# Three changes of order in a two-layer recurrent decoder kernel: an interleaved start, a state output that leaves later, and a spread set-up product

## The chip, the core and the metric

The kernel runs on one core of a Trainium2 chip. The metric is the device time of one execution in microseconds (us); lower is better. The core has a matrix engine (PE, with weight loads shown apart as PEld), a vector engine (DVE), a scalar engine (ACT), a general engine (POOL) and a sync engine (SP), which in this kernel does little but issue DMAs. Each engine works through its own instructions in their order and waits on semaphores where it needs another engine's result.

## The reference, cut

The program computes one inference step of a decoder trunk of two layers for 256 prompt tokens and 8 sequences of 8 sample tokens, 320 columns in all, at a model width of 2048.

```
def _rmsnorm(x, g): return x * lax.rsqrt(jnp.mean(x * x, axis=-1, keepdims=True) + NORM_EPS) * g
...
# per layer, xn = RMSNorm(x), one combined input projection of xn (N_IN = 14336 columns):
#   A: S5      b_bar = ((lam_bar - 1) / lam) * b ; h_t = lam_bar * h_(t-1) + b_bar u_t ; y = c h + d u
#              y = gelu(y) ; y = y * sigmoid(y @ w_glu + b_glu) ; h_last is an output
#   B: RG-LRU  conv of width 4, block-diagonal gates, h_t = a_t h_(t-1) + sqrt(1 - a_t^2) (i_t xc_t)
#   C: RetNet retention, 8 heads, chunks of 128, GroupNorm per head ; the last states are outputs
# x = x + W_out( sum_m sigmoid(gate_m(xn)) * (P_m(branch_m(xn) * silu(z_m))) )
# a final RMSNorm gives y_prompt, y_sample
```

S5 has 64 groups of 16 channels with a complex state of 64 each, and its recurrence runs over the tokens.

## The kernel before, in words

**The stream.** Almost all of the work is dense projections. `blocks()` yields them one after another as blocks of 256 output columns, each with its weights, its number of 128-row pieces of the contraction, the function that gives the moving operand, and the function that evacuates the result. `stream()` cuts the blocks into chunks of four such pieces. There are 312 chunks in a layer, 624 in all. In layer order: input blocks for the RG-LRU's input and gate path and S5's input (48 chunks), the RG-LRU's merge with its gates (48), the retention heads (64), S5's gate path (16), the second merge (48), S5's GLU (8), the third merge (48), the output projection (32).

For every chunk the program loads 512 KB of raw fp32 weights (`load`, L1211, three chunks ahead, into four `raw` buffers, all on SP's queue). In two halves it splits them into a rounded high part (ACT copy, `whi`, L126) and the rest (DVE subtraction, `wlo`, L99), three halves ahead of use (`prep`). PE then does 24 matmuls of 128x320 in three products (L1273 to L1275) into a PSUM tile `pt`. The evacuation of a block is run one chunk after the block's last.

**The background.** Everything else is written as Python generators, which the program advances between chunks: a `yield` means "the rest one chunk later", `yield 2` two chunks later. `step()` advances all of them after each chunk. So a generator's yields set the order of the instructions on every engine, and a wait in it is a loop on a flag that an earlier generator sets, decided when the program is written, not on the chip.

**The parts that the change touches.** `s5_setup` computes S5's discretized input matrix `bb` with 12 products on POOL (`cmul`) and sets the flag on which `s5_weights` and the chain wait. `s5_chain` runs the recurrence over pairs of tokens on POOL, 127 iterations of four small instructions (`cstep`, L555 to L558), in place in `H`. The sample tokens' recurrence is 8 groups of four instructions on DVE (tiles `cb1`, `cb2`), a group in every second step. Behind the last iteration, two POOL copies (L588) gather the last states into `so`, a DMA on SP's queue (L589) writes them out, and `s5_y` follows when the fourth retention pair has its state (the flag `('st', l, 3)`).

At the start, `x_load` brings x in four groups of two DMAs, `x_group` scales it by the norm's weights and splits it, `norm_feed` gathers the sum of squares. The first two blocks run interleaved. `norm_end` sums over partitions on PE (L259) and works out 1/rms, which the blocks' evacuations need. In the last output blocks, `out_proj` sums the squares for the final norm with a matmul by ones (L1081) at block 6 and two more at block 7.

Of the kernel before, what the change touches and what calls it, by code (L numbers as in the profile page):

```python
# [11 lines left out]
F32 = mybir.dt.float32  # L12
# [3 lines left out]
OP = mybir.AluOpType  # L16
# [5 lines left out]
T = SEQ + NB * NS  # L22
# [3 lines left out]
C_U5, C_Z5, C_UL, C_ZL, C_Q, C_K, C_V, C_ZR = (i * W for i in range(8))  # L26
# [54 lines left out]
class Program:  # L81
# [173 lines left out]
    def norm_end(self):  # L255

        yield
        p = self.ps()
        self.nc.tensor.matmul(p[:, :T], self.ones, self.acc, start=True, stop=True)  # L259
        r = self.rstd = self.pl.tile([128, T], F32, name="rstd", tag="rstd")  # L260
        yield from self.rsqrt_steps(p, r)

    def rsqrt_steps(self, p, r):
        v = self.vt([128, T])
        t = self.vt([128, T])
        self.ts(v, p[:, :T], 1.0 / D, OP.mult, EPS, OP.add)
        self.act(t, v, AF.Ln)
        self.act(r, t, AF.Exp, scale=-0.5)
        yield
        self.mul(t, r, r)  # L270
        self.stt(t, t, -0.5, v, OP.mult, OP.mult)
        self.stt(r, t, 1.5, r, OP.add, OP.mult)
# [9 lines left out]

    def x_load(self, q):
        a = self.py.tile([128, 4, T], F32, name="xin", tag="y")
        for h in range(2):
            self.nc.sync.dma_start(a[:, 2 * h:2 * h + 2], self.I['x'][2 * q + h])
        self.xin[q] = a

    def x_group(self, q):

# [29 lines left out]
    def s5_setup(self, l):  # L320
# [10 lines left out]
        B = []  # L331
# [80 lines left out]
        def cmul(r, xr, xi, yr, yi):  # L412
            yr, yi = (v[:, :, None].to_broadcast([128, 32, 16]) for v in (yr, yi))
            o = [t[:, :, :, r] for t in bb]
            g.tensor_tensor(o[0], xr, yr, op=OP.mult)
            g.tensor_tensor(tmp, xi, yi, op=OP.mult)
            g.tensor_tensor(o[0], o[0], tmp, op=OP.subtract)
            g.tensor_tensor(o[1], xi, yr, op=OP.mult)
            g.tensor_tensor(tmp, xr, yi, op=OP.mult)
            g.tensor_tensor(o[1], o[1], tmp, op=OP.add)  # L420
        cmul(1, B[0], B[1], cre, cim)
        cmul(0, bb[0][:, :, :, 1], bb[1][:, :, :, 1], lamr, ni)
        self.bb = bb
        self.flag['bb', l] = True

# [141 lines left out]
    def s5_chain(self, l):  # L567
        nc, H, g = self.nc, self.H, self.nc.gpsimd
        g.memset(H[:, :, :, 0], 0.0)
        lr2 = self.l2r[:, :, None].to_broadcast([128, 32, 2])  # L570
        for j in range(1, HP):
            self.cstep(H[:, :, :, j + 1], H[:, :, :, j], lr2, self.l2i, [128, 32, 2])
        sh = [128, 32, NB]
        cols = H[:, :, :, HP + 1:].rearrange("p q c (b e) -> p q c b e", e=5)
        for i in range(4):
            for c in range(2):
                old, oth, new = cols[:, :, c, :, i], cols[:, :, 1 - c, :, i], cols[:, :, c, :, i + 1]
                t1 = self.vt(sh, name="cb1")
                t2 = self.vt(sh, name="cb2")
                self.mul(t1, old, self.l2r[:, :, None].to_broadcast(sh))  # L580
                self.mul(t2, oth, self.l2i[:, :, c:c + 1].to_broadcast(sh))
                self.add(t1, t1, t2)
                self.add(new, new, t1)
                yield 2
        yield int(HP * 1.43 / 3.26) - 16
        so = self.wt([128, 2, 32, NB + 1], name="so")
        for c in range(2):
            g.tensor_copy(so[:, c], H[:, :, c, HP:HP + 41:5])  # L588
        nc.sync.dma_start(self.O['s5'][l], so)  # L589
        while not self.flag.get(('st', l, 3)):  # L590
            yield
        yield from self.s5_y(l)
        self.flag['s5done', l] = True

# [461 lines left out]
    def out_proj(self, l, j, pt):  # L1056
        nc = self.nc
        xo = self.xo.pop(j)
        if l + 1 < DEPTH:
            self.add(xo, pt[:, :, :T], xo)  # L1060
            nc.sync.dma_start(self.xs[l + 1][j], xo)
            for n in range(2):
                k = 2 * j + n
                self.norm_feed(k, xo[:, n], self.pcol(l + 1, 'norm', k))
            if j == 5:
                self.table_of(AF.Ln)
            if j == 7:
                yield from self.norm_end()
            return
        pool, tag = (self.pmg, "mg") if j % 2 else (self.py, "y")  # L1070
        y = self.ytok[j] = pool.tile([128, 2, T], F32, name="yt", tag=tag)
        if j < 7:
            self.add(y, pt[:, :, :T], xo)
            for n in range(2):
                self.sumsq(y[:, n])
                self.copy(y[:, n], y[:, n], scale=self.pcol(l, 'fin', 2 * j + n))
            if j == 5:
                self.table_of(AF.Ln)
            if j == 6:
                p = self.fsum = self.ps()  # L1080
                self.nc.tensor.matmul(p[:, :T], self.ones, self.acc, start=True, stop=False, skip_group_check=True)  # L1081
            return
        sq = self.wt([128, 2, T], name="sq")
        for n in range(2):
            self.add(y[:, n], pt[:, n, :T], xo[:, n])
            if n:
                self.mul(sq[:, 1], y[:, 1], y[:, 1])
            else:
                self.act(sq[:, 0], y[:, 0], AF.Square)
        for n in range(2):  # L1090
            self.nc.tensor.matmul(self.fsum[:, :T], self.ones, sq[:, n], start=False, stop=n == 1,  # L1091
                                  skip_group_check=True)
# [21 lines left out]
    def blocks(self):  # L1114
        I = self.I
        for l in range(DEPTH):
# [9 lines left out]
            def inp(col, fn, *a):  # L1126
                return (w_in[col // 256], 16, xn, fn, a)

            yield ('call', self.layer_start, (l,))
            for j in range(4):  # L1130
                yield inp(C_UL + 256 * j, self.lru_u, l, j)
                yield inp(C_ZL + 256 * j, self.silu_z, l, self.szl, 'zl', j)
                yield inp(C_U5 + 256 * j, self.s5_u, l, j)
            yield ('call', self.s5_begin, (l,))
            yield from self.merge_blocks(l, 0, inp, wb['lru'], yb, C_GL)
# [22 lines left out]
    def merge_blocks(self, l, br, inp, wb, yb, cg):  # L1158
        def br_blk(j):
            return (wb[j], 8, yb, self.merge, (br, j))  # L1160
        yield inp(cg, self.gate, 0)
        for j in range(1, 8):
            yield inp(cg + 256 * j, self.gate, j)
            yield br_blk(j - 1)
        yield br_blk(7)

    def layer_start(self, l):
        self.nl = 0
# [24 lines left out]
    def stream(self, ahead=3, halves=3):  # L1193
        nc = self.nc
        chunks, calls, nblk = [], {}, 0
        for b in self.blocks():
# [3 lines left out]
            for c in range(b[1] // 4):  # L1200
                chunks.append((nblk, c, b))
            nblk += 1
        first = [x for p in zip(chunks[0:4], chunks[4:8]) for x in p]
        chunks[:8] = first
        raw, hl, pts = {}, {}, {}

        def load(i):
            if i < len(chunks):
                _, c, b = chunks[i]
                t = self.praw.tile([128, 4, 256], F32, name="raw", tag="raw")  # L1210
                nc.sync.dma_start(t, b[0][:, 4 * c:4 * c + 4])  # L1211
                raw[i] = t

        def prep(u):
            i, h = divmod(u, 2)
# [8 lines left out]
        def run(fn, a, now=False):  # L1224
            g = fn(*a)
            if hasattr(g, '__next__'):
                e = self.spawn(g, 0.5 if fn == self.lru_u else 0)
                if now:
                    self.advance(e)
                    e[1] += 1  # L1230
# [3 lines left out]
                run(fn, a)  # L1234

        self.constants()
        self.x_load(0)
        load(0)
        self.more_constants()
        load(1)  # L1240
        self.x_load(1)
        load(2)
        load(3)
        self.x_load(2)
        self.norm_begin()
        for u, _ in enumerate(self.x_group(0)):
            prep(u)
        prep(2)
        self.x_load(3)
        norm = self.norm_end()  # L1250
        done = []
        for i, (nb, c, b) in enumerate(chunks):
            if i:
                load(i + ahead)
            if c == 0:
                call(nb)
                pts[nb] = self.pmain.tile([128, 2, 512], F32, name="pt", tag="pt")
            if i in (1, 3, 4):
                for _ in self.x_group((0, 1, 0, 2, 3)[i]):
                    pass  # L1260
            nk, pt = b[1], pts[nb]
            for h in range(2):
                if (i, h) in ((5, 0), (6, 1), (7, 0)):
                    next(norm, None)
                prep(2 * i + h + halves)
                hi, lo = hl.pop(2 * i + h)
                for n in range(2):
                    for kk in range(2):
                        k = 4 * c + 2 * h + kk
                        xh, xl = b[2](0, k), b[2](1, k)  # L1270
                        o = pt[:, n, :T]
                        cs = slice(n * 128, (n + 1) * 128)
                        nc.tensor.matmul(o, hi[:, kk, cs], xh, start=k == 0, stop=False)  # L1273
                        nc.tensor.matmul(o, hi[:, kk, cs], xl, start=False, stop=False)  # L1274
                        nc.tensor.matmul(o, lo[:, kk, cs], xh, start=False, stop=k == nk - 1)  # L1275
            if i < 5 and i != 2:
                self.x_rest((0, 1, 0, 2, 3)[i])

            if done and i >= done[0][0]:
                run(*done.pop(0)[1:], now=True)  # L1280
            self.step()
            if c == nk // 4 - 1:
                done.append((i + 1, b[3], b[4] + (pts.pop(nb),)))
        for d in done:
            run(*d[1:])
        while self.gens:
# [99 lines left out]
```

## Time and profile before

| | us |
|---|---|
| median of 3 runs | 2486.08 (2485.41 to 2488.9) |
| time of the profiled execution | 2483.85 |
| its span (first to last instruction) | 2482.1 |

| engine | busy us | share | instructions |
|---|---|---|---|
| PE | 2383.9 | 96% | 16762 |
| DVE | 1558.6 | 63% | 2892 |
| ACT | 1068.4 | 43% | 1932 |
| POOL | 618.3 | 25% | 1157 |

The time is 1.75 us above the span, for what lies around the first and last instruction. The shares are averages over the whole span; which engine the others wait for in a stretch has to be read from that stretch.

### The profile page before, as it was taken

Reading aid. Unit: us, or ns where it says so; the run is one execution under the profiler, and the core shown is the slowest. Engines: PE = TensorE matmul, PEld = TensorE weight load, DVE = VectorE, ACT = ScalarE, POOL = GpSimd, SP = SyncE. Lnnn points to the kernel's source line nnn. Section 1 sums busy time; section 2 is a strip of 40 time slices with the busy share of each in tenths; the row PEclk is TensorE's granted clock in tenths of the full one; section 3 lists DMA queues with packets and bytes.
Section 4 is the critical chain, followed back from the end, with each engine's and each line's share of the span. In section 5 each row is a group of like instructions: output and inputs, shape, how many; then the busy total and the mean of one; then the engine's idle time right before and its main releaser. Section 6 shows DMA issues by size and latency. Waiting matters only on the chain. (4 is left out here: it accounts for less than half of the span.)

```text
span 2482.1 us, 44329 instructions
## 1 busy us (share of the span) xinstructions
PE 2383.9 (96%) x16762; PEld 2330.9 (94%) x16762; DVE 1558.6 (63%) x2892; ACT 1068.4 (43%) x1932; POOL 618.3 (25%) x1157
## 2 busy tenths in 40 slices
PE   7999999999599999999999999999959999999996
PEld 7998999999499999999999999999959999999996
DVE  7788557777365656855567665767736647555543
ACT  5654444333133444444455554433323334444443
POOL 2003006999402000300100000799930200000001
PEclk9999999999799999999999999999979999999998
DMA  5654775455254545455555587454434455444553
GB/s 189 190 172 156 213 223 159 152 179 169 77 170 164 190 153 173 151 160 188 188 166 188 161 226 201 150 177 157 134 130 164 155 186 163 150 148 150 162 173 108
DMA packets 153446, 413.71 MB, mean 167 GB/s; under 512 B 18576, under 2 KB 59280, under 8 KB 152976
## 3 DMA queue, kind: packets, MB, share of 16 engines
q1 hardware_dynamic: 152512, 410.58, 52.1%
q8 instruction: 131, 2.15, 0.4%
q14 instruction: 83, 0.68, 0.1%
q10 hardware_dynamic: 720, 0.30, 0.0%
HBM read 373.83 MB, written 31.74 MB: 163 GB/s over the span
## 5 line engine op out<-in xcount | busy, mean ns | idle before, releaser
L99 DVE TENSOR_TENSOR wlo<-raw,whi 128x512 fp32r<-128x512 f32 x1248 | 883.1, 723 | 872.4 <-ACT whi L126 849.9
L126 ACT ACTIVATE whi<-raw 128x512 fp32r<-128x512 f32 x1248 | 776.2, 629 | 1201.9 <-PE pt L1274 1011.8
L1273 PE MATMUL pt<-xh,whi 128*128 128x320 f32 x3584 | 1128.6, 315 | 11.6 <-ACT whi L126 7.3
L1275 PE MATMUL pt<-xh,wlo 128*128 128x320 f32 x3584 | 1112.8, 311 | 7.5 <-DVE wlo L99 7.3
L1274 PE MATMUL pt<-xl,whi 128*128 128x320 f32 x3584 | 1111.7, 310 | 0.0
L1273 PEld LDWEIGHTS pt<-xh,whi 128*128 128x128 f32 x3584 | 676.5, 189 | 26.8 <-ACT whi L126 15.1
L1275 PEld LDWEIGHTS pt<-xh,wlo 128*128 128x128 f32 x3584 | 675.9, 189 | 9.6 <-DVE wlo L99 9.6
L1274 PEld LDWEIGHTS pt<-xl,whi 128*128 128x128 f32 x3584 | 676.5, 189 | 1.7
L1273 PE MATMUL pt<-yhl,whi 128*128 128x320 f32 x768 | 238.8, 311 | 0.0
L1275 PE MATMUL pt<-yhl,wlo 128*128 128x320 f32 x768 | 237.6, 309 | 0.0
L1274 PE MATMUL pt<-yhl,whi 128*128 128x320 f32 x768 | 237.6, 309 | 0.0
L555 POOL TENSOR_TENSOR cs<-H,l2r 128x64 f32<-128x64 f32 x254 | 127.2, 501 | 256.6 <-DVE H L113 236.8
L252 POOL TENSOR_TENSOR acc<-acc,sq 128x320 f32<-128x320 f32 x28 | 25.5, 911 | 609.3 <-ACT sq L126 608.3
L1273 PE MATMUL pt<-M,whi 128*128 128x320 f32 x512 | 159.4, 311 | 0.0
L1275 PE MATMUL pt<-M,wlo 128*128 128x320 f32 x512 | 159.1, 311 | 0.0
L1274 PE MATMUL pt<-M,whi 128*128 128x320 f32 x512 | 159.0, 311 | 0.0
L1273 PEld LDWEIGHTS pt<-yhl,whi 128*128 128x128 f32 x768 | 144.3, 188 | 1.9 <-issue 1.6
L1274 PEld LDWEIGHTS pt<-yhl,whi 128*128 128x128 f32 x768 | 144.3, 188 | 0.0
L1275 PEld LDWEIGHTS pt<-yhl,wlo 128*128 128x128 f32 x768 | 144.2, 188 | 0.0
L558 POOL TENSOR_TENSOR H<-cs,cs 128x64 f32<-128x64 f32 x254 | 128.6, 506 | 19.9
L556 POOL TENSOR_TENSOR cs<-H,l2i 128x64 f32<-128x64 f32 x254 | 127.1, 501 | 0.0
L557 POOL TENSOR_TENSOR cs<-cs,H 128x64 f32<-128x64 f32 x254 | 122.9, 484 | 0.0
(233 smaller groups left out, 2038.0 us busy)
## 6 DMA issues: line engine op xcount, KB each, us to landing
raw<-w_in SPq DMA_DIRECT2D x448, 512.0 KB, 4.4
raw<-w_out SPq DMA_DIRECT2D x64, 512.0 KB, 4.6
raw<-wb_lru SPq DMA_DIRECT2D x32, 512.0 KB, 4.1
raw<-wb_ret SPq DMA_DIRECT2D x32, 512.0 KB, 4.3
raw<-wb_s SPq DMA_DIRECT2D x32, 512.0 KB, 3.6
r<-sret SPq DMA_DIRECT2D x16, 512.0 KB, 7.2
ret_s<-r SPq DMA_DIRECT2D x16, 512.0 KB, 3.0
raw<-w_glu SPq DMA_DIRECT2D x16, 512.0 KB, 3.5
```

Of the source, the lines that this page charges most:

```text
L99: self.nc.vector.tensor_tensor(o, a, b, op=op)
L126: self.nc.scalar.activation(o, a, f, **k)
L252: self.nc.gpsimd.tensor_tensor(self.acc, self.acc, sq, op=OP.add)
L555: g.tensor_tensor(t1, old, lr, op=OP.mult)
L556: g.tensor_tensor(t2, self.swap(old), li, op=OP.mult)
L557: g.tensor_tensor(t1, t1, new, op=OP.add)
L558: g.tensor_tensor(new, t1, t2, op=OP.add)
L1273: nc.tensor.matmul(o, hi[:, kk, cs], xh, start=k == 0, stop=False)
L1274: nc.tensor.matmul(o, hi[:, kk, cs], xl, start=False, stop=False)
L1275: nc.tensor.matmul(o, lo[:, kk, cs], xh, start=False, stop=k == nk - 1)
```

## The change: what it does

It has four parts.

1. **S5's last states.** In `s5_chain`, the copies into `so` stand behind the wait for the flag of the fourth retention pair, and the DMA two steps behind the copies.
2. **The start.** The first three blocks run interleaved, chunk by chunk. The third one accumulates in two PSUM banks of the side pool. The three are evacuated by `unscaled`, which copies the sums out of PSUM on ACT at once, and calls the block's own evacuation when 1/rms is there. The first weight chunk is loaded in two halves, which alternate with the halves of x. The norm's steps are spread a little further, in layer 1 too, and the partition sum stands later in PE's order. In layer 0, `z` comes before `u` in three of the four groups of input blocks, and two gates lead in the first merge.
3. **`cmul`.** After each of the 12 products on POOL there is a `yield`, so they are spread over 12 steps, and what waits for `bb` comes 12 steps later.
4. **The final norm.** The first matmul by ones stands three steps later.

```diff
 def rsqrt_steps(self, p, r):
...
     self.ts(v, p[:, :T], 1.0 / D, OP.mult, EPS, OP.add)
+    yield
     self.act(t, v, AF.Ln)
+    yield
     self.act(r, t, AF.Exp, scale=-0.5)
...
 def cmul(r, xr, xi, yr, yi):
-    g.tensor_tensor(o[0], xr, yr, op=OP.mult)
-    g.tensor_tensor(tmp, xi, yi, op=OP.mult)
-    g.tensor_tensor(o[0], o[0], tmp, op=OP.subtract)
...
+    for i, (a, b) in enumerate(((xr, xi), (xi, xr))):
+        g.tensor_tensor(o[i], a, yr, op=OP.mult)
+        yield
+        g.tensor_tensor(tmp, b, yi, op=OP.mult)
+        yield
+        g.tensor_tensor(o[i], o[i], tmp, op=OP.add if i else OP.subtract)
+        yield
...
 def s5_chain(self, l):
...
     yield int(HP * 1.43 / 3.26) - 16
+    while not self.flag.get(('st', l, 3)):
+        yield
     so = self.wt([128, 2, 32, NB + 1], name="so")
     for c in range(2):
         g.tensor_copy(so[:, c], H[:, :, c, HP:HP + 41:5])
+    yield 2
     nc.sync.dma_start(self.O['s5'][l], so)
-    while not self.flag.get(('st', l, 3)):
-        yield
     yield from self.s5_y(l)
...
         if j == 6:
+            yield 3
             p = self.fsum = self.ps()
...
+def unscaled(self, fn, a, pt):
+    raw = self.wt([128, 2, T], name="un")
+    for n in range(2):
+        self.copy(raw[:, n], pt[n][:, :T])
+    while not self.flag.get('rstd'):
+        yield
+    yield from fn(*a, raw)
...
-    first = [x for p in zip(chunks[0:4], chunks[4:8]) for x in p]
-    chunks[:8] = first
+    chunks[:12] = [chunks[4 * b + q] for q in range(4) for b in range(3)]
...
-    self.x_load(0)
-    load(0)
+    for _ in zip(self.x_load(0), load(0, 2)):
+        pass
```

The first place is SP's queue in the retention heads of layer 0, where the `so` DMA stood before. `raw` is a weight chunk, `rdms`, `rdm` and `rsw` belong to the fourth retention pair, `ret_p` and `ret_s` are its states' outputs. Before:

```order
L1009 DMA ret_p<-rp 128x256
L1211 DMA raw<-w_in 128x1024 x2
L589 DMA s<-so 128x576
L877 DMA rdms<-c_dms 128x64
L879 DMA rdm<-c_dm 128x2x256
L1211 DMA raw<-w_in 128x1024
L834 DMA rsw<-rraw 64x640
```

Of the change, the place in the same queue where the `so` DMA stands now; `k0a<-dk` and `yu<-du` are the first DMAs of `s5_y`:

```order
L1230 DMA raw<-w_in 128x1024 x4
L1031 DMA ret_s<-r_8354 128x1024
L1230 DMA raw<-w_in 128x1024 x3
L597 DMA s<-so 128x576
L604 DMA k0a<-dk 128x1024
L622 DMA yu<-du 128x2x338
L1230 DMA raw<-w_in 128x1024 x3
```

It moved behind the retention's weight loads, from load 156 of layer 0 to load 181 (in layer 1, from load 456 to load 493).

The second place is the start of SP's queue. Before:

```order
L286 DMA xin<-x 128x640 x2
L1211 DMA raw<-w_in 128x1024 x2
L286 DMA xin<-x 128x640 x2
L1211 DMA raw<-w_in 128x1024 x2
L286 DMA xin<-x 128x640 x4
L1211 DMA raw<-w_in 128x1024 x3
```

And with the change:

```order
L290 DMA xin<-x 128x640
L1230 DMA raw<-w_in 128x512
L290 DMA xin<-x 128x640
L1230 DMA raw<-w_in 128x512
L1230 DMA raw<-w_in 128x1024 x2
L290 DMA xin<-x 128x640 x2
L1230 DMA raw<-w_in 128x1024 x3
L290 DMA xin<-x 128x640 x2
L1230 DMA raw<-w_in 128x1024
```

The first half of the first weight chunk stands ahead of the second DMA of x, and the later groups of x stand further back among the weights.

The third place is DVE in layer 0's first retention head, where `ron` are the normalized outputs (read from `ps`) and `wlo` the weights' low parts. Before:

```order
L99 TENSOR_TENSOR ra<-pt,ropr 128x640
L115 TENSOR_SCALAR ron<-ps,mv,gv 128x128 x6
L99 TENSOR_TENSOR wlo<-raw,whi 128x512 x2
L119 SCALAR_TENSOR_TENSOR z<-ps,pv_111,z 128x256
```

And with the change:

```order
L99 TENSOR_TENSOR ra<-pt,ropr 128x640
L115 TENSOR_SCALAR ron<-ps,mv,gv 128x128 x6
L99 TENSOR_TENSOR cb_6256<-H,l2r 128x256
L99 TENSOR_TENSOR cb_6257<-H,l2i 128x256
L99 TENSOR_TENSOR cb_6256<-cb_6256,cb_6257 128x256
L99 TENSOR_TENSOR H<-H,cb_6256 128x32x8
L99 TENSOR_TENSOR wlo<-raw,whi 128x512 x2
```

A group of the sample tokens' recurrence, which stood 12 steps earlier, now stands between the head's work and the next chunk's low parts. Seven more groups follow, one in every second step.

## Rows read from the trace of the kernel before

**Rows 1.** The page: busy time by engine, and its costliest group on DVE.
```profile
PE 2383.9 (96%) x16762; PEld 2330.9 (94%) x16762; DVE 1558.6 (63%) x2892; ACT 1068.4 (43%) x1932; POOL 618.3 (25%) x1157
...
L99 DVE TENSOR_TENSOR wlo<-raw,whi 128x512 fp32r<-128x512 f32 x1248 | 883.1, 723 | 872.4 <-ACT whi L126 849.9
```
**Rows 2.** PE by stretches: stretch, length, busy (instructions), granted clock, DMA share, GB/s.
```profile
0.00:60.00 60.00, 46.65 (x282) 0.97 0.55 188
600.00:900.00 300.00, 270.47 (x2007) 0.95 0.45 149
1800.00:2100.00 300.00, 271.11 (x2042) 0.95 0.48 160
2440.00:2482.10 42.10, 22.24 (x133) 0.80 0.26 95
```
**Rows 3.** PE's timeline: start, duration, instruction, idle time before it and its releaser.
```profile
44.98 0.38 PE L1273 MATMUL pt<-xh,whi 128*128 128x320 f32 x1 [4.34 <-DVE lt L113]
...
219.52 0.63 PE L1275 MATMUL pt<-xh,wlo 128*128 128x320 f32 x1 [4.98 <-DVE wlo L99]
...
664.49 0.77 PE L1020 MATMUL ps<-rvm,rkv 128*128 128x512 f32 x1 [29.53 <-DVE rvm L99]
...
1830.70 0.69 PE L864 MATMUL ps<-ident,rv 128*128 128x128 f32 x2 [28.89 <-DVE r L119]
...
2450.79 0.81 PE L1081 MATMUL ps<-acc,ones 128*128 128x320 f32 x2 [2.79 <-POOL acc L252]
```
**Rows 4.** SP's queue around 654 us, as a timeline: start, duration, DMA issued.
```profile
612.45 3.81 SPq L1211 DMA_DIRECT2D raw<-w_in  x2
...
654.80 0.34 SPq L589 DMA_DIRECT2D s<-so  x1
```
**Rows 5.** POOL's timeline behind the last iteration of layer 0's recurrence.
```profile
653.46 1.32 POOL L588 COPY so<-H 128x288 f32<-128x288 f32 x2
```
**Rows 6.** PE in the stretches behind its waits, columns as in rows 2.
```profile
45.40:48.80 3.40, 3.40 (x15) 0.50 0.66 218
219.50:222.90 3.40, 3.38 (x13) 0.50 0.45 154
664.50:670.00 5.50, 5.50 (x17) 0.50 0.97 298
1830.00:1834.00 4.00, 3.30 (x13) 0.50 0.71 183
2451.80:2455.20 3.40, 3.40 (x15) 0.50 0.00 0
2455.20:2463.00 7.80, 7.80 (x55) 1.00 0.00 0
```
**Rows 7.** All engines around 215 us: busy of PE, PEld, DVE, ACT, POOL; clock, DMA.
```profile
204.40:223.80 19.40, 14.42 (x89) 14.16 (x88) 19.22 (x25) 7.48 (x11) 17.16 (x13) 0.91 0.47 144
```
**Rows 8.** DVE's timeline within it.
```profile
211.58 1.37 DVE L119 SCALAR_TENSOR_TENSOR lr<-lxc,lr 128x344 f32<-128x344 f32 x1
```
**Rows 9.** The same instruction over the whole span: busy us, mean ns.
```profile
L119 DVE SCALAR_TENSOR_TENSOR lr<-lxc,lr 128x344 f32<-128x344 f32 x16 | 10.0, 622 | 0.0
```
**Rows 10.** ACT's timeline at the start.
```profile
4.04 1.01 ACT L126 ACTIVATE xh<-xin,pv 128x320 fp32r<-128x320 f32 x2 [1.38 <-DMA pv<-pv]
...
6.62 0.63 ACT L126 ACTIVATE whi<-raw 128x512 fp32r<-128x512 f32 x1 [1.56 <-DMA raw<-w_in]
```
**Rows 11.** The last instruction of the recurrence's iterations in a stretch of layer 0 (POOL).
```profile
388.00:635.00 247.00, 62.45 (x114) 1.00 0.49 157
```
**Rows 12.** SP's timeline where layer 0's `s5_y` begins.
```profile
748.50 0.78 SPq L598 DMA_DIRECT2D k0a<-dk  x1
```
**Rows 13.** One group of the sample tokens' recurrence on DVE (tiles `cb`).
```profile
444.30:446.70 2.40, 2.27 (x4) 1.00 0.91 307
```
**Rows 14.** DVE in two stretches of layer 0's first retention head.
```profile
471.00:485.00 14.00, 13.86 (x31) 1.00 0.60 177
485.00:499.00 14.00, 11.43 (x17) 1.00 0.50 143
```

More of the change, by code (lines that the diff above doesn't have):

```diff
@@ L261, in norm_end @@
         yield from self.rsqrt_steps(p, r)
+        self.flag['rstd'] = True
     def rsqrt_steps(self, p, r):
@@ L284, in x_load @@
         a = self.py.tile([128, 4, T], F32, name="xin", tag="y")
+        self.xin[q] = a
         for h in range(2):
             self.nc.sync.dma_start(a[:, 2 * h:2 * h + 2], self.I['x'][2 * q + h])
-        self.xin[q] = a
+            yield
     def x_group(self, q):
@@ L414, in cmul @@
             o = [t[:, :, :, r] for t in bb]
-            g.tensor_tensor(o[0], xr, yr, op=OP.mult)
-            g.tensor_tensor(tmp, xi, yi, op=OP.mult)
-            g.tensor_tensor(o[0], o[0], tmp, op=OP.subtract)
[L418 to L422, printed above, removed]
+            for i, (a, b) in enumerate(((xr, xi), (xi, xr))):
[5 more added lines that the diff above has]
+                yield
+        yield from cmul(1, B[0], B[1], cre, cim)
+        yield from cmul(0, bb[0][:, :, :, 1], bb[1][:, :, :, 1], lamr, ni)
         self.bb = bb
@@ L1130, in blocks @@
             for j in range(4):
-                yield inp(C_UL + 256 * j, self.lru_u, l, j)
-                yield inp(C_ZL + 256 * j, self.silu_z, l, self.szl, 'zl', j)
+                two = [inp(C_UL + 256 * j, self.lru_u, l, j), inp(C_ZL + 256 * j, self.silu_z, l, self.szl, 'zl', j)]
+                yield from two[::-1] if l == 0 and j else two
                 yield inp(C_U5 + 256 * j, self.s5_u, l, j)
@@ L1160, in br_blk @@
             return (wb[j], 8, yb, self.merge, (br, j))
[L1161 to L1165, printed above, removed]
+        n = 2 if l == 0 and br == 0 else 1
+        for j in range(8 + n):
+            if j < 8:
+                yield inp(cg + 256 * j, self.gate, j)
+            if j >= n:
+                yield br_blk(j - n)
+    def unscaled(self, fn, a, pt):
[3 more added lines that the diff above has]
+        while not self.flag.get('rstd'):
+            yield
+        yield from fn(*a, raw)
     def layer_start(self, l):
@@ L1202, in stream, with load @@
             nblk += 1
-        first = [x for p in zip(chunks[0:4], chunks[4:8]) for x in p]
-        chunks[:8] = first
+        chunks[:12] = [chunks[4 * b + q] for q in range(4) for b in range(3)]
         raw, hl, pts = {}, {}, {}
-        def load(i):
+        def load(i, parts=1):
             if i < len(chunks):
@@ L1210, in load, with load_all @@
                 t = self.praw.tile([128, 4, 256], F32, name="raw", tag="raw")
-                nc.sync.dma_start(t, b[0][:, 4 * c:4 * c + 4])
                 raw[i] = t
+                n = 4 // parts
+                for h in range(0, 4, n):
+                    nc.sync.dma_start(t[:, h:h + n], b[0][:, 4 * c + h:4 * c + h + n])
+                    yield
+        def load_all(i):
+            for _ in load(i):
+                pass
         def prep(u):
@@ L1226, in run @@
             if hasattr(g, '__next__'):
-                e = self.spawn(g, 0.5 if fn == self.lru_u else 0)
+                e = self.spawn(g, 0.5 if fn in (self.lru_u, self.unscaled) else 0)
                 if now:
@@ L1236, in stream @@
         self.constants()
-        self.x_load(0)
-        load(0)
+        for _ in zip(self.x_load(0), load(0, 2)):
+            pass
         self.more_constants()
[L1240 to L1244, printed above, removed]
-        self.norm_begin()
-        for u, _ in enumerate(self.x_group(0)):
-            prep(u)
+        x = [self.x_load(q) for q in range(1, 4)]
+        for i in range(1, 4):
+            load_all(i)
+            if i == 2:
+                list(x[0])
+        self.norm_begin()
+        group = self.x_group(0)
+        next(group)
+        prep(0)
+        next(group)
+        prep(1)
         prep(2)
-        self.x_load(3)
         norm = self.norm_end()
@@ L1253, in stream @@
             if i:
-                load(i + ahead)
+                load_all(i + ahead)
+            if i in (2, 5):
+                list(x[i // 3 + 1])
             if c == 0:
                 call(nb)
[L1257 to L1260, printed above, removed]
+                if nb == 2:
+                    pts[nb] = [self.ps(), self.ps()]
+                else:
+                    pt = self.pmain.tile([128, 2, 512], F32, name="pt", tag="pt")
+                    pts[nb] = [pt[:, n] for n in range(2)] if nb < 2 else pt
+            if i in (2, 5, 8):
+                list(self.x_group(i // 3 + 1))
             nk, pt = b[1], pts[nb]
             for h in range(2):
-                if (i, h) in ((5, 0), (6, 1), (7, 0)):
+                if 21 <= 2 * i + h <= 25:
                     next(norm, None)
@@ L1270, in stream @@
                         xh, xl = b[2](0, k), b[2](1, k)
-                        o = pt[:, n, :T]
+                        o = pt[n][:, :T] if nb < 3 else pt[:, n, :T]
                         cs = slice(n * 128, (n + 1) * 128)
@@ L1275, in stream @@
                         nc.tensor.matmul(o, lo[:, kk, cs], xh, start=False, stop=k == nk - 1)
-            if i < 5 and i != 2:
-                self.x_rest((0, 1, 0, 2, 3)[i])
+            if i in (1, 3, 6, 9):
+                self.x_rest(i // 3)
             if done and i >= done[0][0]:
@@ L1282, in stream @@
             if c == nk // 4 - 1:
-                done.append((i + 1, b[3], b[4] + (pts.pop(nb),)))
+                pt = pts.pop(nb)
+                if nb < 3:
+                    done.append((i + 1, self.unscaled, (b[3], b[4], pt)))
+                else:
+                    done.append((i + 1, b[3], b[4] + (pt,)))
         for d in done:
```

## The prediction

> **What bounds the kernel now.** I read the page's busy times first. PE is busy 96% of the span, DVE 63% [rows 1]; so the end is set by PE, and a change can win only what PE loses: its idle time, and the time in which it runs at the lower clock. The reader should look next at PE by stretches [rows 2] for where the lost 4% lies, then at its timeline for who ended each long wait [rows 3], and then, since the releaser named is only the last link, at the queue behind that releaser.
>
> Five places hold nearly all of it. In both layers PE stands still in the fourth retention pair, for 29.53 us up to 664.49 and for 28.89 us up to 1830.70 [rows 3]. DVE is named, but SP's queue shows why [rows 4]: the DMA of `so` went out at 654.80, while the weight load ahead of it was dealt with at 612.45, so for some 40 us nothing else left this queue. The `so` DMA was waiting for POOL: the copies into `so` ran from 653.46 for 1.32 us [rows 5], directly behind the last iteration. PE lived on the weights already there until 634.96 and then had none. The third place is a wait of 4.98 us for a `wlo` at 219.52, the fourth one of 4.34 us for the norm's result at 44.98, the fifth one of 2.79 us at 2450.79, for the accumulated squares, ahead of the matmul by ones [rows 3].
>
> Each wait is followed by a stretch in which the granted clock is 0.50 [rows 6], the 1.2 GHz level; behind it, it is 1.00 again (7.80 us for 55 matmuls, so 0.142 us each, against 3.40 us for 15). In such a stretch half of its length is lost: 1.7 us at 45.4, 1.7 at 219.5, 2.75 at 664.5, 1.65 in the 3.30 us of PE work up to 1834, 1.7 at 2451.8.
>
> **The change part by part.** I count in chunks: 24 matmuls at 0.142 us are 3.4 us; the span over 624 chunks is 3.98 us with all stalls in, and some 3.85 without. A step of a generator is that long.
>
> *The states' output.* The `so` DMA now stands behind the fourth pair's states. If POOL has finished by the time SP reaches it, both stalls go, with their low clock: 29.53 + 2.75 = 32.3 us in layer 0 and 28.89 + 1.65 = 30.5 in layer 1. What matters is when the recurrence ends, because part 3 starts it 12 steps later. Before, 114 iterations fell between 388 and 635 [rows 11], 2.17 us each. After: its start moves 12 x 3.85 = 46 us back and 14 us forward (what is saved ahead of it, below), to 420; 127 x 2.17 = 275 us lead to 695, and the copies to 697. The new place is directly ahead of `k0a<-dk`, which went out at 748.50 [rows 12]: less 32.3 and 14 saved, plus two steps (7.7) and the 3 lost below, this is 713. A margin of 16 us, and three chunks (11 us) of loaded weights before PE would feel a wait. In layer 1 the recurrence keeps its place and the DMA goes back by 37 loads, some 140 us, against a wait of 40. I take the whole 62.8.
>
> *`cmul`.* Around 215 us DVE is busy 19.22 of 19.4 us and POOL 17.16 of them, with 13 instructions [rows 7]; an RG-LRU instruction of DVE takes 1.37 us there [rows 8] against 0.622 in the mean of all [rows 9]. So the 12 products, back to back, slow DVE until `wlo` is late. Spread over 12 steps, one product of 17.16/13 = 1.32 us comes in each 3.85 us, and DVE's mean load of 63% leaves 1.4 us. Gain 4.98 + 1.7 = 6.7 at the most, nothing at the least; I take 6.2, nearly all, because what is left of the wait cannot be much longer than one product.
>
> *The start.* PE is idle 60 - 46.65 = 13.35 us of the first 60 [rows 2]. ACT made the first `whi` at 6.62 after waiting 1.56 us for `raw`, and took 0.63 [rows 10], so PE began at about 7.3; half of the bytes first should save most of that wait, 1.3. The wait for the norm (4.34 + 1.7) goes, because three interleaved blocks are 12 chunks (some 41 us) and none of them needs the norm to leave PSUM. The other 1.7 us of small waits (13.35 - 7.3 - 4.34) stay or go. Against it stand six more ACT copies of 320 columns, 0.5 us each by the like of 1.01 us for two [rows 10], on an engine at 43%; if they push `whi` back, they cost up to 3. I take 7.3, with 4 to 9 as bounds.
>
> *The final norm.* Moved behind the last block's matmuls, the matmul by ones waits for nothing: 2.79 + 1.7 are gained at 2450.79 and the low clock at 2451.8. The 0.81 us of that pair stay but fall between the last weights and the last squares, when PE waits for DVE anyway. Together 5.3; at the least 2.8, if low clock comes at another place.
>
> *What is new.* The sample tokens' recurrence moves onto the first retention head of layer 0. A group costs DVE 2.27 us [rows 13], and there are two in 14 us (four chunks), 4.5 us. DVE is busy 13.86 of the first 14 us there and 11.43 of the next [rows 14]. The first four chunks overflow by 13.86 + 4.5 - 14 = 4.4 us, the next by 2.0; in all 6.4. Halves are prepared three ahead, 3 x 1.9 = 5.7 us, less 0.63 for ACT's copy [rows 10] and 0.72 for the subtraction [rows 1]: a lead of 4.4. So PE waits 2.0 us, with a low clock behind it another 1. I take 3 lost; the bounds are 0 (DVE's work there need not be urgent) and 8 (all of the backlog, and 1.7 of clock).
>
> The other moves (`z` before `u`, two gates ahead, two more yields in the norm of layer 1) shift DVE and ACT work by one or two chunks where these are at 63% and 43% [rows 1]. Zero, within 1 us.
>
> Sum: 32.3 + 30.5 + 6.2 + 7.3 + 5.3 - 3 = 78.6 us. Against the profiled execution's 2483.85 (span 2482.1, 1.75 around it) this gives 2405.2. The median of the runs shown, 2486.08, is 2.2 higher, so on their scale it is **2407 us**.
>
> **The rivals.**
>
> *B: the wait for `so` comes back in layer 0.* With the start at 420, SP waits if an iteration takes over (713 - 420 - 1.3)/127 = 2.30 us, and PE if over 2.38, when the loaded weights are used up. For it: in the new place the recurrence shares its whole time with DVE work of the retention heads, at 14 us per 13.86 of DVE [rows 14]. Against it: 2.17 is measured over most of those same heads. At 2.45 us it would cost 9 us and 2 of clock, about 2418.
>
> *C: the spread products disturb DVE as much as before.* Each still meets DVE: at a load above (3.85 - 1.32)/3.85 = 66% a step doesn't hold both, and 19.22 of 19.4 [rows 7] is far above, though that load contains the waiting itself. Then the 6.2 are not gained, and the start may keep half of its loss as well: 2413 to 2417. The Trainium skill, "SBUF — State Buffer", section "Who interferes with whom", says that a VectorE instruction with two SBUF inputs and a GpSimd instruction that reads SBUF take an exclusive lock on a shared port pair, and that the loser is blocked for the whole instruction. By that rule the 1.37 us against 0.622 is blocking, spreading leaves the sum of it as it was, and only the step's slack decides, which gives the time of this rival where there is none.
>
> *D: DVE's new load costs 8 us, not 3.* For it the 13.86 of 14 us [rows 14]; against it the lead of 4.4 us. It gives 2412.
>
> *E: slower than before.* The recurrence in layer 0 is slowed by DVE to 3.0 us an iteration: it would end at 420 + 381 + 1 = 802, 78 us behind the 724 at which PE runs dry, which eats the gain. From 3.0 us on the sum has the other sign, at 3.1 it gives about 2500. Against it: 2.17 us is the mean of 247 us under the same kind of load [rows 11].
>
> *F: nothing comes of it,* if SP waits at the new place for as long as at the old. The order rules that out for layer 1, and for layer 0 it is the narrow band of E around 3.0 us.
>
> **How the numbers follow.** The forecast has 0.68 (its own range 2401 to 2411), B 0.10, C and D together 0.18, E 0.02, and F with all that I can't name 0.02. The range from 2399 to 2418 takes in C, D and the cheap half of B. All but E and F are faster by far more than the 0.2% (5 us) that a measurement of this kernel can tell from no change: faster 0.97, same 0.01, slower 0.02.
>
> **What would show it.** Right: no PE wait above 5 us in 600 to 900 and 1800 to 2100, and `so` leaving SP a few tenths behind the load ahead of it; no wait for the norm near 45; no low clock near 215 and no `wlo` wait there; the first matmul before 6.5 us; the two last squares' matmuls directly behind the matmul by ones. Wrong: POOL's copies into `so` later than 713 in layer 0, waits for `wlo` in the first retention head above 5 us, or a `whi` late by the copies of the first three blocks. The forecast fails as a whole if the weight loads themselves, at the DMA share of 0.45 to 0.48 in the two stretches [rows 2], could not follow without the stalls; I see no sign of that.

## The result, and the profile after

The changed kernel takes 2413.13 us (median of 4 runs, 2412.17 to 2413.35) against 2486.76 us beside it: a ratio of 0.970, with a 95% interval of 0.969 to 0.972. The forecast was 2407 within 2399 to 2418. The profiled execution gained 70.5 us (2483.85 to 2413.35) where the sum had 78.6.

The page after, and PE by stretches (stretch, length, busy, granted clock, DMA share, GB/s), beside [rows 1, 2]:

```profile
PE 2377.8 (99%) x16762; PEld 2325.6 (96%) x16762; DVE 1566.0 (65%) x2892; ACT 1076.0 (45%) x1941; POOL 635.6 (26%) x1157
```
```profile
0.00:60.00 60.00, 53.65 (x353) 1.00 0.62 214
160.00:220.00 60.00, 54.47 (x346) 0.97 0.47 147
455.00:500.00 45.00, 39.78 (x249) 0.96 0.42 126
600.00:900.00 300.00, 300.00 (x2226) 1.00 0.49 165
1750.00:2050.00 300.00, 300.00 (x2248) 1.00 0.51 169
```

The two stretches with the long stalls are full to the last tenth. The start has lost nothing but the time to the first matmul. What is left lies in two places, 160 to 220 and 455 to 500, and PE's timeline after shows the waits in them (`rvm` is an operand of the retention's state matmuls, which DVE makes). With two more of 0.8 us at 181 and 186, and two of 0.2 us directly behind the `rvm` matmuls shown here, these are all of PE's waits above 0.15 us:

```profile
6.35 0.64 PE L1303 MATMUL pt<-xh,whi 128*128 128x320 f32 x1 [6.35 <-ACT whi L126]
...
177.06 0.41 PE L1305 MATMUL pt<-xh,wlo 128*128 128x320 f32 x1 [0.81 <-DVE wlo L99]
...
207.18 0.41 PE L1303 MATMUL pt<-xh,whi 128*128 128x320 f32 x1 [1.04 <-ACT whi L126]
209.80 0.41 PE L1305 MATMUL pt<-xh,wlo 128*128 128x320 f32 x1 [2.05 <-DVE wlo L99]
468.14 0.42 PE L1305 MATMUL pt<-xh,wlo 128*128 128x320 f32 x1 [1.19 <-DVE wlo L99]
475.69 0.47 PE L1026 MATMUL ps<-rvm,rkv 128*128 128x512 f32 x1 [1.98 <-DVE rvm L99]
487.14 0.47 PE L1026 MATMUL ps<-rvm,rkv 128*128 128x512 f32 x1 [1.53 <-DVE rvm L99]
2394.21 1.34 PE L1098 MATMUL ps<-sq,ones 128*128 128x320 f32 x4 [0.55 <-ACT sq L126]
```

Behind two of them the clock is down, as in [rows 6]; the last row is a stretch at full clock where it was down before:

```profile
211.30:214.70 3.40, 3.40 (x15) 0.51 0.60 183
477.20:480.60 3.40, 3.40 (x15) 0.54 0.43 133
2380.00:2392.90 12.90, 12.90 (x90) 1.00 0.00 2
```

The recurrence in layer 0 ended where it was forecast (695 and 697 for the copies, 713 for the DMA), 18 us ahead of its DMA. POOL's timeline and SP's after:

```profile
695.11 1.84 POOL L595 COPY so<-H 128x288 f32<-128x288 f32 x2 [0.16 <-POOL H L563]
```
```profile
715.40 0.42 SPq L597 DMA_DIRECT2D s<-so  x1
```

The products of part 3 had not spread. In POOL's timeline after, the twelve run nearly without a gap, from 195.14 to 213.86. Two of them before, then the second, the third and the last two after:

```profile
218.79 1.60 POOL L418 TENSOR_TENSOR bb<-bb,lamr 128x512 f32<-128x512 f32 x1
220.35 1.53 POOL L419 TENSOR_TENSOR s5bt<-bb,lami 128x512 f32<-128x512 f32 x1
```
```profile
197.92 1.06 POOL L422 TENSOR_TENSOR s5bt<-s5b,s5t 128x512 f32<-128x512 f32 x1 [1.34 <-ACT li L126]
199.06 1.64 POOL L424 TENSOR_TENSOR bb<-bb,s5bt 128x512 f32<-128x512 f32 x1
...
210.63 1.53 POOL L422 TENSOR_TENSOR s5bt<-bb,lami 128x512 f32<-128x512 f32 x1
212.24 1.62 POOL L424 TENSOR_TENSOR bb<-bb,s5bt 128x512 f32<-128x512 f32 x1
```

### The profile page after: what moved, and what is told of

The parts are those of the page before. It is cut to its first block, busy times and chain, and to the rows that moved or that the text cites. A ratio compares the mean times of both kernels' runs of the same rounds, so it can differ in the third digit from the quotient of the medians.

```text
span 2411.6 us, 44360 instructions
## 1 busy us (share of the span) xinstructions
PE 2377.8 (99%) x16762; PEld 2325.6 (96%) x16762; DVE 1566.0 (65%) x2892; ACT 1076.0 (45%) x1941; POOL 635.6 (26%) x1157
## 4 chain that ended last, share of the span: by engine, by line
PE 79%; DVE 0%; ACT 0%; issue 0%; ACTq 0%; DVEq 0%
PE pt L1303 25%; PE pt L1305 24%; PE pt L1304 24%; PE ps L1027 1%; PE ps L634 0%; PE ps L757 0%; PE ps L640 0%; PE ps L945 0%; PE ps L1026 0%; PE ps L543 0%; DVE yt L99 0%; PE ps L1001 0%; PE ps L894 0%; PE ps L947 0%; PE ps L941 0%; PE ps L487 0%
## 5 line engine op out<-in xcount | busy, mean ns | idle before, releaser
L1303 PE MATMUL pt<-xh,whi 128*128 128x320 f32 x3552 | 1115.2, 314 | 7.5 <-ACT whi L126 7.4
L1305 PE MATMUL pt<-xh,wlo 128*128 128x320 f32 x3552 | 1100.3, 310 | 5.7 <-DVE wlo L99 5.7
L1304 PE MATMUL pt<-xl,whi 128*128 128x320 f32 x3552 | 1099.3, 309 | 0.0
L1303 PEld LDWEIGHTS pt<-xh,whi 128*128 128x128 f32 x3552 | 668.9, 188 | 21.4 <-ACT whi L126 14.1
L1305 PEld LDWEIGHTS pt<-xh,wlo 128*128 128x128 f32 x3552 | 668.6, 188 | 7.3 <-DVE wlo L99 7.2
L1304 PEld LDWEIGHTS pt<-xl,whi 128*128 128x128 f32 x3552 | 669.0, 188 | 1.7
L560 POOL TENSOR_TENSOR cs<-H,l2r 128x64 f32<-128x64 f32 x254 | 133.1, 524 | 256.7 <-DVE H L113 237.0
L562 POOL TENSOR_TENSOR cs<-cs,H 128x64 f32<-128x64 f32 x254 | 130.8, 515 | 0.0
```

What stands on the lines that cost most here:

```text
L560: g.tensor_tensor(t1, old, lr, op=OP.mult)
L562: g.tensor_tensor(t1, t1, new, op=OP.add)
```

## The experiments

**The yields between the products.** The changed kernel, with the products as they were:

```diff
-                g.tensor_tensor(o[i], a, yr, op=OP.mult)
-                yield
...
+            g.tensor_tensor(o[0], xr, yr, op=OP.mult)
+            g.tensor_tensor(tmp, xi, yi, op=OP.mult)
...
```

> The changed kernel with the 12 products on POOL without yields between them, as before the change. Theory P (a yield between them paces nothing on the chip, since POOL has no other work in its order and starts each product when its operands are there; it only delays what waits for the result): the products lie where they lay, back to back from about 195 us, the waits of PE there stay (about 3 us and the low clock), the sample tokens' groups go back by 12 steps, out of the first retention head, and the 5.1 us of waits with 1.6 us of low clock in 455 to 500 go: about 2406.5 us. Theory Q (the yields do spread the products, and 3 us of wait are what is left of 5 because a step has too little slack): the wait near 205 grows to 5 us, and the time is 2409 to 2410.

2406.97 us (2406.4 to 2407.76), 6.2 less than with the change. PE by stretches: nothing is lost any more in 455 to 500, while the wait at 211 is one of 3.08 us. The low clock begins within it here, and 4.67 us of PE's work lie in it, for 3.4 with the change:

```profile
209.20:216.00 6.80, 4.67 (x17) 0.51 0.32 90
455.00:500.00 45.00, 45.00 (x300) 1.00 0.50 153
```

So theory P holds: the products lie where they lay, with the yields or without. The 1 us between 2.05 and 3.08, and about 0.6 of low clock, belong to neither theory; what makes them is not shown.

**Products that are spread on the chip.** Ahead of each product, in its own step, ACT writes one column and POOL reads it:

```diff
...
+            def pace():
+                n = self.ntok = self.ntok % 24 + 1
+                self.copy(self.tok[:, n - 1:n], self.fv[:, 3, 1:2])
+                g.tensor_copy(self.tok2, self.tok[:, n - 1:n])
...
+                pace()
                 g.tensor_tensor(o[i], a, yr, op=OP.mult)
                 yield
...
```

> The changed kernel, with a small ACT copy in each of the 12 steps that POOL must wait for ahead of its product, so that the products are spread on the chip and not only in the order. Theory P: products one per 3.5 to 4 us from 195 on, no wait of PE above 1 us in 195 to 245: 2408 to 2409 us. Theory Q (each product blocks DVE by its whole length wherever it lies, and DVE has no slack at about 90% busy): waits of 2 to 4 us, spread over 195 to 245, and 2411 to 2414 us.

2407.99 us (2407.55 to 2408.54), 5.1 less than the change, as by theory P. POOL now waits for ACT ahead of eight of the products, and the twelve lie between 207 and 245, some still in twos and threes. POOL's timeline, and PE, which has no wait there:

```profile
207.03 0.19 POOL L426 COPY tok<-tok 128x1 f32<-128x1 f32 x1 [11.89 <-ACT tok L126]
207.18 1.07 POOL L429 TENSOR_TENSOR bb<-s5b,s5t 128x512 f32<-128x512 f32 x1
211.12 0.19 POOL L426 COPY tok<-tok 128x1 f32<-128x1 f32 x1 [2.88 <-ACT tok L126]
211.26 1.06 POOL L432 TENSOR_TENSOR s5bt<-s5b,s5t 128x512 f32<-128x512 f32 x1
```
```profile
195.00:245.00 50.00, 50.00 (x343) 1.00 0.59 182
```

**The products left out.**

```diff
...
+            for i in range(2):
+                if r:
+                    g.memset(bb[i], 0.0)
+                for _ in range(3):
+                    yield
...
```

> The changed kernel without the 12 products (the matrix bb is set to zero by two POOL instructions, so S5's input is left out; all steps and all that follows stay). It bounds what any spreading could win. If the products cause the waits at 205 to 210: none there, wlo at its usual 0.65 us, 2408 us; the same in layer 1 changes nothing. If the waits come from DVE's own work at this place (it is 94 to 96% busy already at 170 to 190, without any product, with 2.4 us of waits): 1 to 3 us of wait stay and the time is 2410 to 2413. The waits at 177 to 186 stay by either.

2408.23 us (2408.21 to 2408.86): spreading the products costs no more than not having them. All engines (PE, PEld, DVE, ACT, POOL) in 194 to 214, first after the change, then without the products:

```profile
194.00:214.00 20.00, 16.91 (x105) 16.38 (x104) 18.70 (x27) 10.21 (x17) 17.38 (x14) 0.93 0.52 159
```
```profile
194.00:214.00 20.00, 20.00 (x138) 20.00 (x137) 13.62 (x35) 15.55 (x26) 3.35 (x7) 1.00 0.70 210
```

With the products DVE is busy for 18.70 us with 27 instructions, without them for 13.62 with 35. It is the same subtraction that takes longer beside a product; DVE's timeline with the products, and without:

```profile
198.19 1.34 DVE L99 TENSOR_TENSOR wlo<-raw,whi 128x512 fp32r<-128x512 f32 x1 [0.40 <-ACT whi L126]
199.71 1.54 DVE L99 TENSOR_TENSOR wlo<-raw,whi 128x512 fp32r<-128x512 f32 x1 [0.17 <-ACT whi L126]
```
```profile
198.47 0.69 DVE L99 TENSOR_TENSOR wlo<-raw,whi 128x512 fp32r<-128x512 f32 x1 [0.43 <-ACT whi L126]
199.99 0.69 DVE L99 TENSOR_TENSOR wlo<-raw,whi 128x512 fp32r<-128x512 f32 x1 [0.83 <-ACT whi L126]
```

The Trainium skill, "SBUF — State Buffer", section "Who interferes with whom", has the one of the two engines blocked for the other's whole instruction. The added 0.65 and 0.85 us agree with that kind of blocking, within products of 1.06 to 1.68 us.

Pacing does not take this cost away. DVE in 190 to 280, first without the products, then with paced ones, is busy 7.8 us longer with them for the same number of instructions:

```profile
190.00:280.00 90.00, 53.55 (x109) 1.00 0.52 159
```
```profile
190.00:280.00 90.00, 61.34 (x109) 1.00 0.52 159
```

PE has no wait with the paced ones, so here DVE's slack takes the cost.

**The sample tokens' groups, further apart.** `yield 4` for `yield 2` between the groups.

> The changed kernel with four steps instead of two between the eight groups of the sample tokens' recurrence. If the sum of DVE work in a step is what makes PE wait in 455 to 500 (2.27 us of a group on top of 13.9 and 11.4 us of 14): the waits of 5.1 us fall to 1 or 2 and the low clock goes: 2407 to 2409 us. If it is one instruction that comes late (the rvm that PE waits for stands behind a group, wherever the group is): the waits are as long, only at other heads, and the time stays at 2412 to 2414.

2421.2 us (2419.63 to 2422.18), 8.1 more than the change: neither expectation. PE's waits are hardly longer in sum (18.7 us against 17.5 over the span), but behind three of them PE now works at the low clock for longer. Two of these waits, and the stretches behind them:

```profile
485.27 0.77 PE L1026 MATMUL ps<-rvm,rkv 128*128 128x512 f32 x1 [2.49 <-DVE rvm L99]
...
560.18 0.76 PE L1026 MATMUL ps<-rvm,rkv 128*128 128x512 f32 x1 [1.96 <-DVE rvm L99]
```
```profile
485.40:491.90 6.50, 6.50 (x21) 0.50 0.02 4
560.20:567.00 6.80, 6.80 (x22) 0.50 0.02 7
```

The third stands behind the wait at 210, which is as long as in the change (2.06 us for 2.05), and PE works in it for 5.4 us. These 6.7, 6.8 and 5.4 us at half clock lose 9.5 us, the change's two times 3.4 lose 3.4; with the waits' 1.2 this is 7.3, of 7.7 between the two profiled executions. About 1 us of it, at 210, lies far ahead of the groups and can't be theirs. Spread over twice the time, the groups met the next head as well: the wait at 560 is for its `rvm`.

**The parts one by one, on the kernel before.** First part 1 alone.

> The kernel before with part 1 alone: the states' copies behind the fourth retention pair, their DMA two steps later. If the two stalls of PE are SP's wait for the copies and nothing else: no wait of PE above 1 us in the fourth pair of either layer, and 62.8 us less than before (29.5 + 28.9 of waits, 4.4 of low clock), about 2423 us. If another wait stands behind that one (the weight loads at their rate, the next pair's operands): 5 to 20 us of the waits stay, 2428 to 2443.

2422.26 us (2420.26 to 2424.16), 62.1 less than before's 2484.38 beside it. PE by stretches, where both stalls had been [rows 2]:

```profile
600.00:900.00 300.00, 300.00 (x2238) 1.00 0.50 164
1750.00:2050.00 300.00, 300.00 (x2244) 1.00 0.52 172
```

Two things elsewhere nearly cancel: the first matmul comes at 8.85 us for 7.30, and the wait ahead of the matmul by ones (2.80 us) has no low clock behind it here, which was 1.7 us.

Part 2 alone:

> The kernel before with part 2 alone (the start, with the norm's steps and the new order of layer 0's first blocks). By the profile of the change it is worth 1.0 of an earlier first matmul, 6.1 of waits and 1.7 of low clock in the first 60 us; the waits near 180 and 210 are as in the run with the products back to back (2.4 and 4.1 us, 3.4 of low clock), against 5.8 and 1.7 before, so that 2 to 3 us are given back: 2479 to 2480 us. If the start alone is what counts: 2477.

2473.98 us, ratio 0.9959 (0.9945 to 0.9974): 10 us less, with an interval of some 4 us to either side. That is more than either expectation. The first 60 us are as in the change:

```profile
0.00:60.00 60.00, 53.70 (x349) 1.00 0.63 214
```

Around the products it won nothing (waits of 3.08 and 1.04 us and three of 0.8, for 4.98, 0.64 and 0.81 before). But the wait of 2.79 us ahead of the matmul by ones, which is still there, again has no low clock behind it: 1.7 us of the gain lie there, far from the start.

Part 3 alone:

> The kernel before with part 3 alone (the yields between the products). If they pace nothing on the chip and only delay what follows: the wait of about 5 us near 219 stays, the recurrence of layer 0 starts some 45 us later, the states' DMA, still at its old place, waits longer by the time of the 21 iterations that no longer fit ahead of PE's stop (21 x 1.4 us = 30), and the first retention head gets the waits of the change (5 us and 1.7): about 2520 us, clearly slower than before. If they do spread the products: 5 to 7 us less than that.

2475.32 us, ratio 0.9964 (0.9951 to 0.9977): faster by 9 us, where I had expected 35 more. The wait near 219 did stay (5.00 us), and the first head has its waits. But the DMA's old place is counted in steps from the recurrence's start, so it went back by 12 steps too, and these steps, in the retention heads, last longer than the 12 of the recurrence's start: the DMA left 46.4 us later than before (654.80 [rows 4]), while PE ran dry 59.8 us later (at 694.80, for 634.96). SP's timeline, and PE's:

```profile
701.22 0.34 SPq L590 DMA_DIRECT2D s<-so  x1
```
```profile
219.34 0.64 PE L1276 MATMUL pt<-xh,wlo 128*128 128x320 f32 x1 [5.00 <-DVE wlo L99]
...
709.30 0.77 PE L1021 MATMUL ps<-rvm,rkv 128*128 128x512 f32 x1 [14.50 <-DVE rvm L99]
```

Layer 0's stall is 14.50 us for 29.53 [rows 3]: 15.0 won there, 6.9 lost in the first head (5.2 of waits, 1.7 of low clock), together 8.1 of the 9. My expectation had moved the recurrence and left its DMA where it was.

**The change without part 1,** which rests on that reading:

```diff
         yield int(HP * 1.43 / 3.26) - 16
-        while not self.flag.get(('st', l, 3)):
-            yield
         so = self.wt([128, 2, 32, NB + 1], name="so")
...
```

> The changed kernel without part 1: the states' copies and their DMA at their old place, directly behind the recurrence's last step in program order, which part 3 has moved by 12 steps in layer 0. If the stall is as long as the recurrence ends behind the moment at which PE runs dry: as in the run with part 3 alone, 14 to 15 us in layer 0 and 29 in layer 1, with 2 to 4 us of low clock behind each: 2459 to 2464 us. If part 1 is worth what it is worth by itself: 62.1 us more, 2475.

2462.11 us (2458.97 to 2464.61), with waits of 11.58 us in layer 0 and 30.60 in layer 1: the time is as expected, though layer 0's wait is some 3 us shorter and layer 1's 1.6 longer than that. It is 49.0 more than the change, so part 1 is worth 62 alone and 49 beside the other parts.

**The change without part 4** (`yield 3` taken away):

> The changed kernel without part 4 (the first matmul by ones at block 6 again, three steps earlier). If part 4 is worth its wait, its low clock and the pair of matmuls that it takes off the path, as forecast: 5.3 us more, 2418 us. If the pair at the end, now behind the last weights, delays the end by its own 0.7 us: 4.6 more.

2418.11 us (2418.08 to 2419.68), 5.0 more. The wait is back, at its old length:

```profile
2385.06 1.43 PE L1087 MATMUL ps<-acc,ones 128*128 128x320 f32 x2 [2.79 <-POOL acc L252]
```

**Paced products, and the groups out of the head.** First with S5's set-up 12 steps earlier (`yield 2` for `yield 14` ahead of it in `first_setup`):

> The changed kernel with paced products, as in the second run, and S5's set-up spawned 12 steps earlier in layer 0, so that the recurrence and the sample tokens' groups keep the place that they had before the change. If the two costs are separate (products that come together, and groups that land on the first retention head): neither the waits near 205 nor those in 455 to 500, about 2402 to 2403 us. If DVE at the set-up's new place (some 40 us earlier, also 80% busy) can't hold it: new waits of 2 to 5 us near 130 to 180, 2405 to 2409.

2406.02 us (2405.82 to 2406.47). The waits in 455 to 500 are gone, but the paced products now lie between 161 and 212, and two of them between 188 and 191.4. DVE's two `wlo` take 2.39 us there, for 1.29 in the run without the earlier set-up, and PE waits:

```profile
190.26 0.41 PE L1316 MATMUL pt<-xh,wlo 128*128 128x320 f32 x1 [2.48 <-DVE wlo L99]
```

It stands behind the expected 130 to 180; the time is in the band of the second case.

Then with the groups parted around the head's dense stretch:

```diff
                 self.add(new, new, t1)
-                yield 2
+                yield (2, 11, 1)[(2 * i + c > 2) + (2 * i + c > 3)] if l == 0 else 2
```

> The changed kernel with paced products, and with the sample tokens' groups in layer 0 set around the first retention head's dense stretch: four before it (as they stand), eleven steps of pause, the other four one step apart in the lighter stretch behind it (DVE 8.4 to 10 us of 15 there). If what decides is DVE's load at the place where the groups fall: no wait in 455 to 500 nor behind it, 4.9 us of waits and 1.7 of low clock less than with paced products alone, 2401 to 2402 us. If groups one step apart overload the lighter stretch as well: waits near 500 to 530 and 2405 to 2409.

2400.2 us (2400.15 to 2400.87), 12.9 less than the change, ratio to before 0.966 (0.965 to 0.967): the fastest of all. PE by stretches:

```profile
160.00:220.00 60.00, 57.54 (x381) 1.00 0.53 160
421.00:511.00 90.00, 90.00 (x645) 1.00 0.51 163
```

Only the three waits of 0.8 us near 180 remain between the first matmul and the last squares.

## Why the prediction was right, and where it was off

The time came out 6 us above the forecast, inside the range. By its terms:

- *The states' output* (62.8): right. 58.4 us of waits and the low clock behind them are gone; part 1 alone gives 62.1. The recurrence was forecast from 420 to 695 and the DMA for 713; it began at 419.61, its copies at 695.11, and the DMA left at 715.40. The 2.17 us per iteration held. Rivals B and E fell with that.
- *`cmul`* (6.2): wrong. The step that failed is "Spread over 12 steps, one product of 17.16/13 = 1.32 us comes in each 3.85 us". A step is a place in the program's order; POOL has no other instruction there to wait behind, so it ran all twelve as soon as their operands were ready. Part 3 won nothing at its own place, and its delay put the sample tokens' groups onto the first head. Undone, it gives back 6.2 us. Rival C had the outcome and half of the reason: what the products cost DVE does stay when they are spread (7.8 us with paced ones), but DVE has the slack for it, once they are really apart. The waits from 160 on are 5.5 us after the change (up to 220) and were 6.4 before (up to 226: 0.64, 4.98 and 0.81). Three of 0.8 us near 180 are new, and are there without the products as well. Part 2 alone has them, parts 1 and 3 alone don't; and with S5's set-up 12 steps earlier they stand 45 us earlier, at 132 to 142. So they seem to come where the set-up's own work on DVE meets part 2's new order.
- *The start* (7.3): right, a little low. 7.0 us of waits (13.35 less 6.35) and 1.7 of low clock, 8.7. The ACT copies of the first blocks delayed nothing: behind the first matmul PE has no wait in the first 60 us. Which piece of part 2 earns how much was not tested apart.
- *The final norm* (5.3): right; 5.0 by its run. The time alone doesn't tell 5.3 from 4.6, but the trace does: with the pair at the end, PE's wait ahead of the last squares falls from 1.09 us to 0.55, so the pair hides.
- *The first head* (3 lost): mis-sized. It lost 5.1 us of waits and 1.7 of low clock, 6.8, near the bound of 8 and rival D. The lead of 4.4 us was counted for `wlo`, but two of the three long waits are for `rvm`, which the sum did not have. DVE makes it one step ahead of its use, and the first of the two directly behind a group:

```profile
472.57 0.61 DVE L99 TENSOR_TENSOR cb<-H,l2r 128x256 f32<-128x256 f32 x1
...
474.75 1.54 DVE L99 TENSOR_TENSOR rvm<-rkv,sm 128x512 fp32r<-128x512 f32 x2
```

PE's matmul started at 475.69.

With these, 62.8 + 0.9 + 8.7 + 5.3 - 6.8 = 70.9, against 70.5 measured. The miss is 5.3 from part 3, 3.8 from the head, less 1.4 from the start.

## What to carry to other kernels

Spacing instructions out in program order paces only an engine that has other instructions between them. An idle engine runs them together at the old time, and the delay falls on what waits for the result; to spread them on the chip, let each wait for something that its own step produces. Spreading does not make them cheaper for the engine beside them; it lets that engine's slack take them. And when a delayed step reappears elsewhere, check both what it now lies beside and what is placed relative to it: here a DMA moved along, and a vector group landed on an engine that was already full.

## What the runs showed of the hardware that I had not expected

What a short wait of PE costs varied more than the wait itself. Waits of 0.8 us, one of 1.05 and one of 1.53 left the granted clock at 1.00. Behind most waits of 1.9 to 3.1 us it fell to 0.50, the 1.2 GHz level, and PE then worked for 3.4 to 6.8 us in it. A wait of 1.98 us thus cost 3.7 us in the change, and one of 1.96 us cost 5.4 with the groups further apart.

The length of the wait does not decide it. The wait of 2.79 us ahead of the matmul by ones had the low clock behind it in the kernel before [rows 6] and in the change without part 4. With part 1 alone the same wait (2.80 us) had none, and with part 2 alone (2.79) none either. In the change without part 1, a wait of 1.31 us in the first head had 3.4 us of it; with paced products the one of 1.32 us there had none. PE with part 1 alone, behind the wait of 2.80, and in the change without part 1, behind that of 1.31:

```profile
2390.00:2396.00 6.00, 6.00 (x40) 1.00 0.00 0
```
```profile
490.00:493.40 3.40, 3.40 (x13) 0.50 0.03 5
```

So the 1.7 us that the prediction adds to each wait is what the trace of the kernel before shows, and not a fixed price; differences of 1 to 3 us between two of these kernels can come from it alone. What decides, these runs don't settle.
